# Some weight pages used unsplit in a four-phase transformer kernel: one expert page in eight, every second page of the u table

## The chip, the cores and the metric

The kernel runs on one core of a Trainium2 chip. The metric is the device time of one execution in microseconds (us). Before the change it is 3914.66 us, the median of 3 runs (3913.98 to 3925.19).

Names of the profile: PE is TensorE's matmuls, PEld its weight loads, DVE is VectorE, ACT is ScalarE, POOL is GpSimd, SP is the engine that issues loads. PEclk is the clock granted to TensorE as a share of its full speed.

## The reference

512 tokens of width 1024 go through two layers: attention, a mixture of 32 experts, a state-space model beside a second attention, and a PEER feed-forward. All inputs are float32. The change touches the mixture and the PEER part:

```
def expert_block(args):            # a block of tokens of expert e
    xe, e = args
    gu = xe @ w_gate_up[e] + b_gate_up[e]
    g = jnp.minimum(gu[:, :D_FF], SWIGLU_LIMIT)
    u = jnp.clip(gu[:, D_FF:], -SWIGLU_LIMIT, SWIGLU_LIMIT)
    act = (u + 1.0) * (g * jax.nn.sigmoid(SWIGLU_ALPHA * g))
    return act @ w_down[e] + b_down[e]

# PEER: 8 heads, 16 best of 128 x 128 experts for each token
s_top, i_top = lax.top_k(scores, PEER_TOPK)
best_s, pos = lax.top_k(cand_s, PEER_TOPK)
expert_idx = jnp.take_along_axis(cand_i, pos, axis=-1)
gates = jax.nn.softmax(best_s, axis=-1)
u_sel = u_tab[i_blk]
act = jax.nn.gelu(jnp.einsum('td,thkd->thk', h_blk, u_sel))
w = g_blk * act
out = jnp.einsum('thk,thkd->td', w, v_tab[i_blk])
```

## The kernel before

The program has four phases, one after the other on the same engines: attention (to about 490 us), experts (490 to 1852), state-space model and second attention (1852 to 2464), and PEER (from 2464). Nearly all instructions are recorded through one helper, so they carry line 84 (`Timed.call`); they are told apart by their tiles' names.

**Pages.** Weights come as pages of 128 x 1024 float32 (512 KB), loaded on SP's queue (`WStream.load`, L213) into a buffer `wr`. `WStream.split1` (L217) makes two buffers of each: `wh`, its rounding to the short float32r form, copied by ScalarE, and `wl` = `wr` - `wh`, a subtraction on VectorE or, where the stream's function `eng` says so, on GpSimd. `Kern.mm3` (L167) then multiplies exactly enough with three products: high by high, high by low, low by high. `wr`, `wh` and `wl` are buffers of one pool, which come free when their last reader is done; `ahead` (L238) and `get` (L265) load and split a number of pages ahead of use.

**Experts** (`Expert`, L1216 to L1322; `expert_stream`, L1349; `phase2`, L1375). An expert has 24 pages in the stream: 8 gate/up pages of its first half of columns, the 8 down pages of the expert before it, 8 gate/up pages of its second half. A page's product goes to two PSUM banks of 128 x 512 (`gu` or `dn`), three products each, so six matmuls a page. The 128 tokens of an expert are gathered by GpSimd (`xg`), transposed by TensorE and split (`transpose_x`, L1248: `exh`, `exl`); the activations likewise (`transpose_act`, L1286: `ath`, `atl`). Expert number `HOME` has a second block of 128 tokens, multiplied with the same pages; so 33 blocks are computed from 32 experts' pages. A loop for still more blocks (`Overflow.rest`, L1515) is in the program and is run zero times with these inputs. Every sixth page's `wl` is GpSimd's (L1372). The order of everything is written out in `phase2`: page by page, with the other steps at set page numbers.

**PEER, first stage (the u stage, 2464 to 3390).** `norm_T` (L1834) transposes and splits the normed input into `HT`. A stream of 16 query pages and 128 pages of the u table follows (L2234 to L2238). A query page gives 24 products of 512 columns; a u page (`uchunk`, L2297) gives 24 products of 384 columns (three blocks of 128 tokens) into a bank `ft`, which ScalarE turns into `us` and stores to DRAM (`Sd`). Beside this run `select` (L2320), which picks the 16 best of 50 candidate pairs for each head (a one-hot `oh` of 128 x 800, made by VectorE, multiplied with the indices `ci` at L2352 and reduced), and `gates` (L2387), which builds for each token one-hots `oa` and `oB` of 128 columns and multiplies them on TensorE (`G`), in float32 without a split. Three in four `oB` are VectorE's, the fourth is ScalarE's. The fourth block of tokens takes another way: `gathered` (L2445) fetches rows of the tables with indirect DMAs from POOL's queue and adds them up on VectorE.

The order of the u stage is made by `race` (L99): it interleaves these lanes by a table of estimated durations (`Clock`, L33). The same estimates choose, through `Clock.either` (L42), VectorE or GpSimd for each `wl` of a u page and for each multiplication of `oh`. The order and the choice are fixed when the program is built.

**PEER, second stage (the v stage, 3390 to 3917).** `vphase` (L2504) goes through 128 pages of the v table, each split as above, with 18 products of 512 columns into six banks `out` that stay open to the end. Pages of this phase come from a pool of 10 buffers (`open_pages`, L2629).

Of the kernel before, what the change touches and what calls it, by code (L numbers as in the profile page):

```python
# [15 lines left out]
ALU = mybir.AluOpType  # L16
# [16 lines left out]
class Clock:  # L33
    """Estimates when each engine gets done with what has been emitted for it; race() orders the steps of several lanes by it."""
# [4 lines left out]
    def __init__(self):  # L39
        self.start()  # L40

    def either(self, n, bias=0.0):  # L42
        """the one of VectorE and GpSimdE that gets done first with so many columns"""
        cost = [max(self.free[e], self.floor) + self.FIXED[e] + n * self.ELEM[e] for e in ("vector", "gpsimd")]
        return "vector" if cost[0] + bias < cost[1] else "gpsimd"
# [17 lines left out]
class Timed:  # L63
    """An engine whose instructions are told to the clock."""
# [34 lines left out]
def race(clock, *gens):  # L99
    """Interleaves lanes, the step that comes due first first. A lane may yield the time its next step has to wait for;  # L100
    else that is the end of its last step."""
# [94 lines left out]
class WStream:  # L196
    """Weight pages: loaded ahead, split into exact float32r halves ahead of their use."""

    def __init__(self, K, srcs, load_ahead, split_ahead, queue=None, shape=None, eng=None, late=False):
        self.eng = eng or (lambda i: None)  # L200
        self.K, self.srcs = K, list(srcs)
# [15 lines left out]
    def split1(self):  # L217
        if self.isp < len(self.srcs):
# [3 lines left out]
            self.raw[self.isp] = None  # L222
            hi = self.K.page(F32R, shape=self.shape, name="wh")
# [8 lines left out]
    def low(self):  # L232
        """the low halves of what has been split."""
# [12 lines left out]
    def lane(self, ahead, n=None):  # L246
        """splits as a lane of its own, so many pages ahead of the use."""
# [11 lines left out]
    def next(self):  # L259
        """get(), when it has been split."""  # L260
# [15 lines left out]
def weave(*gens):  # L276
    """gens: (generator, steps per unit of time, start); interleaves their steps."""
# [28 lines left out]
def phase1(K):  # L306
# [36 lines left out]
    # first modulation by blocks of columns, so that the first products start early  # L343
# [24 lines left out]
    # row norms of x, the scaled rows' transpose  # L368
# [14 lines left out]
    def mod_block(k):  # L383
        """sum over the rows of w_ada of one block of columns, shift and scale."""
# [54 lines left out]
    def product(bs, k, w):  # L439
        """one row block's part of a half chunk: two blocks of tokens to a bank."""  # L440
# [8 lines left out]
    def normed(c, half):  # L449
        """queries and keys with their heads' norms."""  # L450
# [19 lines left out]
    def drain(c, half, bs):  # L470
        """bs: the blocks of tokens in PSUM, pairs of them or one with all columns."""
# [22 lines left out]
    def take(**n):  # L494
        """waits until so much of the space is free, in the order of the program."""
# [23 lines left out]
    # the first chunk, as the blocks of the modulation come in  # L519
# [37 lines left out]
    def prep(c0, p, out):  # L557
        """q^T and k^T of a pair of heads of 64, split; the gains go with q."""
# [20 lines left out]
    def scores(qk, biases, den, es):  # L579
        """exponentials of the scores of two heads, less each row's maximum, and their sums."""  # L580
# [29 lines left out]
    def weigh(todo, new):  # L610
        """todo: per head its exponentials, the split values' columns, and PSUM [query, block, columns] or the output's place."""
# [50 lines left out]
    def out_pair(b, k, r=slice(0, P)):  # L662
        """a pair's output, transposed in PSUM, split for the output projection."""
# [9 lines left out]
    def pair_a(p):  # L673
# [25 lines left out]
        # each head with the values of both; its own half of the rows is kept  # L699
# [78 lines left out]
    def mods2():  # L778
        """gate and second modulation as rows, broadcast over the partitions."""
# [50 lines left out]
    # output projection: first with the differential heads, then with the others  # L830
# [30 lines left out]
    def projects():  # L861
        """output projection: the differential heads' part, that of the first pairs of the others, and what is left with the second norm"""
# [25 lines left out]
    def third(tb):  # L888
        """the last part of the projection, the residual's squares"""
# [1755 lines left out]
```

## Time and profile before

| | |
|---|---|
| median of 3 runs | 3914.66 us |
| profiled execution, its span | 3917.8 us |
| PE busy | 3450.1 us, 88% |
| DVE busy | 3368.7 us, 86% |
| ACT busy | 1848.5 us, 47% |
| POOL busy | 1761.6 us, 45% |
| DMA, mean | 231 GB/s |

The profile gives one execution, on the hardware profiler's clock; its own time is its span, 3917.8 us, 3.1 us above the median of the runs. A busy time is a sum over instructions. Where an instruction stands still inside itself, waiting for a port or for data, that is in its busy time too. Matmuls are pipelined: a matmul's own duration is longer than the spacing to the next, so the cost of one is read from the time that many take. A float32 product that is not of the rounded halves is recorded as two matmuls.

### The profile page before, as it was taken

To read this page: it belongs to the slowest core of one execution; us is meant where nothing else is said; L and a number is where in the kernel's file an instruction comes from. 1 tells how busy PE (TensorE), PEld (TensorE's weight loads), DVE (VectorE), ACT (ScalarE), POOL (GpSimd) and SP (SyncE) were. 2 spreads that over 40 slices of the span, in tenths; PEclk is the share of its full clock that TensorE was granted. 3 is DMA by queue.
4 is the path that set the end of the run, shared out by engine and by line. 5 is a ranking of instruction groups with operands and counts; after the bars stand their busy time and mean duration, and the time that the engine had idled before them with its cause. 6 is when DMAs were issued, how large, how long until landed. Compare 5 with 4: busy or idle time off the path is not lost. (4 is left out here: it accounts for less than half of the span.)

```text
span 3917.8 us, 52046 instructions
## 1 busy us (share of the span) xinstructions
PE 3450.1 (88%) x17053; PEld 2921.3 (75%) x17053; DVE 3368.7 (86%) x5450; ACT 1848.5 (47%) x2684; POOL 1761.6 (45%) x1021
## 2 busy tenths in 40 slices
PE   6887689888989999998489899899688889999999
PEld 6776577666778777776377777788678789988887
DVE  7887799999997999997688774589999996598888
ACT  3334266665765767675234343433334445333333
POOL 6554434323332333332344340266666564555554
PEclk8878799999999999999699999899888999999999
DMA  6224379888987999997511122366568686999997
GB/s 213 85 83 146 127 263 316 299 301 282 321 293 245 320 338 328 338 330 254 175 49 49 49 61 89 124 220 214 187 209 262 210 298 211 328 343 340 344 342 264
DMA packets 453989, 906.04 MB, mean 231 GB/s; under 512 B 37810, under 2 KB 188978, under 8 KB 453586
## 3 DMA queue, kind: packets, MB, share of 16 engines
q1 hardware_dynamic: 333488, 692.66, 52.1%
q0 software_dynamic: 46368, 151.03, 11.0%
q10 hardware_dynamic: 73858, 59.00, 4.5%
q8 instruction: 135, 2.21, 0.2%
q14 instruction: 140, 1.15, 0.1%
HBM read 845.42 MB, written 74.96 MB: 235 GB/s over the span
## 5 line engine op out<-in xcount | busy, mean ns | idle before, releaser
L84 DVE TENSOR_TENSOR wl<-wr,wh 128x1024 fp32r<-128x1024 f32 x855 | 1210.4, 1445 | 113.9 <-ACT wh L84 106.5
L84 ACT CAST wh<-wr 128x1024 fp32r<-128x1024 f32 x1133 | 1133.3, 1049 | 206.1 <-POOL wl L84 53.4
L84 POOL TENSOR_TENSOR wl<-wr,wh 128x1024 fp32r<-128x1024 f32 x278 | 714.3, 2570 | 809.8 <-ACT wh L84 695.1
L84 PE MATMUL ft<-HT,wh 128*128 128x384 f32 (+1 forms) x2304 | 637.6, 359 | 2.4 <-ACT wh L84 2.0
L84 PE MATMUL gu<-wl,exh 128*128 128x512 f32 x1056 | 426.9, 404 | 88.1 <-DVE wl L84 81.6
L84 PE MATMUL out<-wh,HT 128*128 128x512 f32 x1536 | 473.2, 389 | 1.8 <-ACT HT L84 1.5
L84 PEld LDWEIGHTS ft<-HT,wh 128*128 128x128 f32 x2304 | 438.8, 200 | 12.5 <-ACT wh L84 2.4
L84 PE MATMUL ft<-HT,wl 128*128 128x384 f32 (+1 forms) x1152 | 409.6, 356 | 34.6 <-POOL wl L84 24.0
L84 PE MATMUL gu<-wh,exh 128*128 128x512 f32 x1056 | 423.6, 401 | 0.0
L84 PE MATMUL gu<-wh,exl 128*128 128x512 f32 x1056 | 417.4, 395 | 0.0
L84 PEld LDWEIGHTS out<-wh,HT 128*128 128x128 f32 x1536 | 288.2, 188 | 62.3 <-ACT HT L84 1.8
L84 PEld LDWEIGHTS gu<-wl,exh 128*128 128x128 f32 x1056 | 201.3, 191 | 162.8 <-DVE wl L84 116.0
L84 PE MATMUL out<-wl,HT 128*128 128x512 f32 x768 | 298.8, 389 | 0.0
L84 PEld LDWEIGHTS ft<-HT,wl 128*128 128x128 f32 x1152 | 228.6, 198 | 46.9 <-POOL wl L84 28.6
L84 DVE TENSOR_SCALAR oa<-iota,rt 128x128 f32<-128x128 f32 x384 | 227.1, 595 | 19.8 <-PE G L84 19.6
L84 PE MATMUL qkv<-wl,hTh 128*128 128x256 f32 (+1 forms) x736 | 227.1, 308 | 14.5 <-DVE wl L84 11.9
L84 PE MATMUL qkv<-wh,hTh 128*128 128x256 f32 (+1 forms) x736 | 234.7, 319 | 2.0 <-ACT wh L84 2.0
L84 PEld LDWEIGHTS gu<-wh,exh 128*128 128x128 f32 x1056 | 201.6, 191 | 44.5 <-issue 1.5
L84 PEld LDWEIGHTS gu<-wh,exl 128*128 128x128 f32 x1056 | 201.3, 191 | 39.9
L84 PE MATMUL qkv<-wh,hTl 128*128 128x256 f32 (+1 forms) x736 | 226.2, 307 | 2.5 <-DVE hTl L84 2.5
L84 PE MATMUL dn<-wl,ath 128*128 128x512 f32 x528 | 210.2, 398 | 11.0 <-DVE wl L84 9.6
L2454 POOL DMA_INDIRECT ug<-in_peer_v,et x128 | 153.9, 1202 | 139.5 <-DVE x L84 74.0
(482 smaller groups left out, 7054.1 us busy)
## 6 DMA issues: line engine op xcount, KB each, us to landing
wr<-in_w_gate_up SPq DMA_DIRECT2D x512, 512.0 KB
wr<-in_w_down SPq DMA_DIRECT2D x256, 512.0 KB
wr<-in_u_t SPq DMA_DIRECT2D x128, 512.0 KB
wr<-in_peer_v SPq DMA_DIRECT2D x128, 512.0 KB
wr<-in_w_in SPq DMA_DIRECT2D x68, 512.0 KB
wada<-in_w_ada SPq DMA_DIRECT2D x48, 512.0 KB
Sd<-us ACTq DMA_DIRECT2D x128, 192.0 KB
Gd<-gst ACTq DMA_DIRECT2D x12, 2048.0 KB
```

What stands on the lines that cost most here:

```text
L84: return f(*a, **kw)
L2454: nc.gpsimd.indirect_dma_start(out=r, out_offset=None, in_=tab, in_offset=bass.IndirectOffsetOnAxis(ap=et[:, m:m + 1], axis=0), bounds_che ...
```

## The change

- `WStream` gets a function `whole`: for a page that it names, nothing is split and the raw page is handed to the user.
- Experts: pages with number 5 of each eight are used unsplit (`WHOLE`), 3 of 24 in each expert. `gu_page` and `down_page` then do one plain float32 product for each bank instead of three. The input's slice for it is kept unsplit (`Expert.keep`, an extra ScalarE copy `un` of 128 x 128). The function `eng` is gone, so all low halves of the experts are VectorE's. The loop in `Overflow.rest` likewise.
- u table: odd pages, 64 of 128, are used unsplit, with one float32 product of 384 columns for each of the eight parts instead of three. The unsplit input stands in `HW`, which `norm_T` fills with eight more ScalarE activations. The other u pages' low halves are all VectorE's.
- The multiplication of `oh` is always VectorE's.
- `us` has three buffers instead of four; the pool of the last phase has 8 page buffers instead of 10.
- Comments and docstrings are dropped (left out below).

```diff
 class WStream:
-    def __init__(self, K, srcs, load_ahead, split_ahead, queue=None, shape=None, eng=None, late=False):
+    def __init__(self, K, srcs, load_ahead, split_ahead, queue=None, shape=None, eng=None, late=False, whole=None):
         self.eng = eng or (lambda i: None)
+        self.whole = whole or (lambda i: False)
...
             self.raw[self.isp] = None
+            if self.whole(self.isp):
+                self.done.append((r,))
+                self.isp += 1
+                return
             hi = self.K.page(F32R, shape=self.shape, name="wh")
...
+WHOLE = (5,)
...
             K.split(b, self.xT[0][:, s], self.xT[1][:, s])
+            self.keep(self.xw, b, half)
+
+    def keep(self, out, b, half):
+        for k in WHOLE:
+            if k // 4 == half:
+                out[k] = self.K.small([P, P], tag=f"un{k}", bufs=6)
+                self.K.nc.scalar.copy(out[k], b[:, k % 4 * P:(k % 4 + 1) * P])
...
     def gu_page(self, k, w):
         s = slice(k * P, (k + 1) * P)
         for i in range(2):
+            if len(w) == 1:
+                self.K.nc.tensor.matmul(self.gu[i], self.xw[k], w[0][:, i, :], start=False, stop=k == KC - 1)
+                continue
...
     def down_page(self, k, w):
...
+            if len(w) == 1:
+                self.K.nc.tensor.matmul(self.dn[i], self.aw[k], w[0][:, hs], start=k == 0, stop=k == KC - 1)
+                continue
...
-    K.ws = WStream(K, srcs, MLA[0], 3, eng=lambda i: K.nc.gpsimd if i % 6 == 5 else None)
+    K.ws = WStream(K, srcs, MLA[0], 3, whole=lambda i: i % KC in WHOLE)
...
-def norm_T(K, x, gcol, outs, scratch_gain=True):
+def norm_T(K, x, gcol, outs, whole=None):
...
+        if whole is not None:
+            n = whole.shape[2]
+            nc.scalar.activation(whole[:, k, :], b[:, 0:n], AF.Copy, scale=gcol[:, k:k + 1])
...
-    ws = WStream(K, [(flat if c else feat)(n) for c, n in order], 3, 2, eng=lambda i: getattr(nc, K.clock.either(D, VB)) if order[i][0] else None)
+    ws = WStream(K, [(flat if c else feat)(n) for c, n in order], 3, 2, whole=lambda i: order[i][0] and order[i][1] % 2)
...
+    HW = K.const([P, KC, TD], name="HW")
+    xn = norm_T(K, K.x3, gcol, hTk, HW)
...
         for k in range(KC):
+            if len(w) == 1:
+                nc.tensor.matmul(b[:, 0:n], w[0][:, k, :], HW[:, k, 0:n], start=k == 0, stop=k == KC - 1)
+                continue
...
-        s = K.small([P, TD], tag="us", bufs=4)
+        s = K.small([P, TD], tag="us", bufs=3)
...
-                getattr(nc, K.clock.either(TK * NCAND, VB2)).tensor_tensor(out=oh, in0=oh, in1=ci[:, h, None, :].to_broadcast(sh), op=ALU.mult)
+                v.tensor_tensor(out=oh, in0=oh, in1=ci[:, h, None, :].to_broadcast(sh), op=ALU.mult)
...
-            K.open_pages(K.ctx4, 10)
+            K.open_pages(K.ctx4, 8)
```

What the change does to the order of instructions, at three places. TensorE, page 5 of the first expert's down product. `dn` are the two banks, `wh` and `wl` the halves of the page, `ath` and `atl` those of the activations, `wr` the raw page, `un` the slice kept unsplit. Before, page 5 and the first product of page 6:

```order
L84 MATMUL dn_4652<-wh_4672,ath_4217 128x512
L84 MATMUL dn_4652<-wl_4673,ath_4217 128x512
L84 MATMUL dn_4652<-wh_4672,atl_4218 128x512
L84 MATMUL dn_4653<-wh_4672,ath_4217 128x512
L84 MATMUL dn_4653<-wl_4673,ath_4217 128x512
L84 MATMUL dn_4653<-wh_4672,atl_4218 128x512
L84 MATMUL dn_4652<-wh_4692,ath_4217 128x512
```

and now, from the last product of page 4 on:

```order
L84 MATMUL dn_4635<-wh_4642,atl_4220 128x512
L84 MATMUL dn_4634<-wr_4556,un_4596 128x512
L84 MATMUL dn_4635<-wr_4556,un_4596 128x512
L84 MATMUL dn_4634<-wh_4670,ath_4219 128x512
L84 MATMUL dn_4634<-wl_4671,ath_4219 128x512
```

Six products became two, which need the raw page and no low half.

POOL in the u stage, late, where the gathers (`ug`, indirect DMAs) run. Before, they stand between low halves and multiplications:

```order
L2454 DMA ug_24511<-in_peer_v,et_22053 128x1024
L84 TENSOR_TENSOR wl_24537<-wr_24364,wh_24536 128x1024
L2454 DMA ug_24570<-in_peer_v,et_22053 128x1024
L2454 DMA ug_24600<-in_peer_v,et_22053 128x1024
L84 TENSOR_TENSOR wl_24606<-wr_24431,wh_24605 128x1024
L2454 DMA ug_24659<-in_peer_v,et_22053 128x1024
L84 TENSOR_TENSOR wl_24665<-wr_24472,wh_24664 128x1024
L84 TENSOR_TENSOR oh_24699<-oh_24699,ci_24519 128x800
```

and now the gathers are alone:

```order
L2483 DMA ug_23613<-in_peer_v,et_21394 128x1024
L2483 DMA ug_23657<-in_peer_v,et_21394 128x1024
L2483 DMA ug_23716<-in_peer_v,et_21394 128x1024
L2483 DMA ug_23739<-in_peer_v,et_21394 128x1024
L2483 DMA ug_23781<-in_peer_v,et_21394 128x1024
```

In the whole program POOL's subtractions `wl` went from 278 to 27 (all 27 in the first phase) and its multiplications `oh` from 28 to 0.

VectorE at the same place, in a selection: `bpf` are the positions found, `x` is the sum of gathered rows, `ex` the reduced indices. Before:

```order
L84 CAST bpf_24579<-bp_24578 128x128
L84 TENSOR_TENSOR oh_24699<-bpf_24579,iotac_21953 128x800
L84 SCALAR_TENSOR_TENSOR x_21923<-ug_24350,sv_22824,x_21923 128x1024
L84 TENSOR_TENSOR oh_24741<-bpf_24579,iotac_21953 128x800
L84 TENSOR_TENSOR oh_24741<-oh_24741,ci_24519 128x800
L84 SCALAR_TENSOR_TENSOR x_21923<-ug_24511,sv_22824,x_21923 128x1024
L84 TENSOR_REDUCE ex_24520<-oh_24699 128x16
```

and now:

```order
L84 CAST bpf_23636<-bp_23635 128x128
L84 TENSOR_TENSOR oh_23736<-bpf_23636,iotac_21285 128x800
L84 TENSOR_TENSOR oh_23736<-oh_23736,ci_23596 128x800
L84 SCALAR_TENSOR_TENSOR x_21255<-ug_23452,sv_22081,x_21255 128x1024
L84 TENSOR_TENSOR oh_23744<-bpf_23636,iotac_21285 128x800
L84 TENSOR_TENSOR oh_23744<-oh_23744,ci_23596 128x800
L84 TENSOR_TENSOR wl_23748<-wr_23620,wh_23747 128x1024
```

Every multiplication stands right behind its one-hot now, and a low half `wl` of a u page stands in VectorE's order too.

## Rows read from the trace of the kernel before

**Rows 1.** Windows view: stretch, length, busy us of each engine, PEclk, DMA share, GB/s.

```profile
490.00:1852.00 1362.00, 1248.90 (x5562) 991.85 (x5560) 1292.10 (x1599) 897.75 (x1036) 460.70 (x198) 0.98 0.88 304
2464.00:3390.00 926.00, 808.10 (x4426) 766.29 (x4427) 796.45 (x1958) 364.48 (x645) 550.83 (x303) 0.93 0.68 222
3390.00:3917.00 527.00, 522.53 (x2304) 431.98 (x2303) 461.94 (x425) 189.50 (x256) 290.75 (x233) 1.00 0.93 329
1600.00:1800.00 200.00, 186.05 (x849) 149.67 (x849) 195.77 (x199) 142.47 (x166) 70.18 (x30) 1.00 0.95 330
2689.00:3214.00 525.00, 430.26 (x2307) 410.57 (x2308) 515.12 (x1078) 203.58 (x382) 342.61 (x192) 0.90 0.70 229
```

**Rows 2.** Groups by shape, 490 to 1852: count, busy us, mean ns, idle before, releasers.

```profile
L84 DVE TENSOR_TENSOR wl<-wr,wh 128x1024 fp32r<-128x1024 f32 x637 | 900.8, 1452 | 20.1 <-ACT wh L84 17.2 <-DMA ybuf<-y,dst 1.8
...
L84 PE MATMUL gu<-wl,exh 128*128 128x512 f32 x1056 | 426.9, 404 | 88.1 <-DVE wl L84 81.6 <-POOL wl L84 6.1
...
L84 POOL TENSOR_TENSOR wl<-wr,wh 128x1024 fp32r<-128x1024 f32 x128 | 344.1, 2689 | 516.6 <-ACT wh L84 473.8 <-PE dn L84 15.7 <-PE gu L84 14.2
...
L84 PE MATMUL dn<-wl,ath 128*128 128x512 f32 x528 | 210.2, 398 | 11.0 <-DVE wl L84 9.6 <-POOL wl L84 1.2
...
L84 DVE SCALAR_TENSOR_TENSOR act<-swu,swt 128x512 f32<-128x512 f32 x66 | 80.2, 1214 | 3.1
...
L84 DVE SCALAR_TENSOR_TENSOR swt<-gu,swr 128x512 f32<-128x512 f32 x66 | 45.1, 684 | 2.4 <-ACT swr L84 2.4
```

**Rows 3.** Timeline (start, duration, engine) around 2902 us, and VectorE's at 1303 us.

```profile
2901.86 0.28 DVE L84 TENSOR_SCALAR oB<-iota,rt 128x128 f32<-128x128 f32 x1
2902.06 0.34 DVE L84 TENSOR_SCALAR oa<-iota,rt 128x128 f32<-128x128 f32 x1
...
2902.16 2.53 POOL L84 TENSOR_TENSOR wl<-wr,wh 128x1024 fp32r<-128x1024 f32 x1 [6.21 <-ACT wh L84]
2902.32 2.46 DVE L84 TENSOR_SCALAR oB<-iota,rt 128x128 f32<-128x128 f32 x1
...
1303.31 2.36 DVE L84 TENSOR_TENSOR wl<-wr,wh 128x1024 fp32r<-128x1024 f32 x2
```

**Rows 4.** Groups by shape, 2464 to 3390 (columns as in rows 2).

```profile
L84 PE MATMUL ft<-HT,wl 128*128 128x384 f32 x1024 | 358.0, 350 | 24.1 <-POOL wl L84 24.0
L84 POOL TENSOR_TENSOR wl<-wr,wh 128x1024 fp32r<-128x1024 f32 x123 | 302.6, 2461 | 185.9 <-ACT wh L84 142.3 <-issue 30.2 <-PE G L84 8.3
...
L84 DVE TENSOR_SCALAR oa<-iota,rt 128x128 f32<-128x128 f32 x384 | 227.1, 595 | 19.8 <-PE G L84 19.6 <-ACT rt L84 0.2
L84 DVE TENSOR_SCALAR oB<-iota,rt 128x128 f32<-128x128 f32 x288 | 163.5, 568 | 0.0
...
L84 PE MATMUL G<-oB,oa 128*128 128x128 f32 x768 | 129.3, 304 | 67.3 <-DVE oB L84 62.4 <-ACT oB L84 3.5
...
L84 ACT ACTIVATE us<-ft 128x384 f32<-128x384 f32 x128 | 62.9, 491 | 240.5 <-PE ft L84 236.5 <-DMA wr<-in_u_t 2.1 <-issue 1.7
L84 POOL TENSOR_TENSOR oh<-oh,ci 128x800 f32<-128x800 f32 x28 | 59.4, 2126 | 89.3 <-DVE oh L84 86.3 <-DMA wr<-in_u_t 3.0
...
L84 DVE TENSOR_TENSOR oh<-oh,ci 128x800 f32<-128x800 f32 x4 | 4.0, 992 | 0.1
```

**Rows 5.** The chain of waits near the end of the u stage: start, us, what.

```profile
3256.55 0.89 PE G L84 x8
3257.44 4.16 PE ft L84 x24
```

**Rows 6.** Timeline of PE in the third phase, float32 products of 512 columns.

```profile
2203.96 1.90 PE L84 MATMUL y<-tmp,cz 128*32 128x512 f32 x4
```

**Rows 7.** Timeline of PE, the bias products that open two successive experts.

```profile
1706.03 0.63 PE L84 MATMUL gu<-bg,pls 128*128 128x512 f32 x2
...
1745.34 0.63 PE L84 MATMUL gu<-bg,pls 128*128 128x512 f32 x2
```

**Rows 8.** Waits of SP's DMA queue, 3391 to 3900: us in total, times, longest.

```profile
SPq L213 <- PE out L84: 347.0, 118, 3.2
```

More of the change, by code (lines that the diff above doesn't have):

```diff
@@ L1221, in __init__ @@
         self.sel = sel
+        self.xw, self.aw = {}, {}
     def slots(self):
@@ L1293, in transpose_act @@
         K.split(b, self.aT[0][:, s], self.aT[1][:, s])
+        self.keep(self.aw, b, c)
     def down_start(self):
@@ L1521, in rest @@
             srcs = [gu_src(self.wgu, c, k) for c in range(2) for k in range(KC)] + [self.wdn[k * P:(k + 1) * P, :] for k in range(KC)]
-            ws = WStream(K, srcs, 6, 3)
+            ws = WStream(K, srcs, 6, 3, whole=lambda i: i % KC in WHOLE)
             x.slots()
@@ L2246, in hTk @@
         return HT[0][:, k, 0:n], HT[1][:, k, 0:n]
-    xn = norm_T(K, K.x3, gcol, hTk)
+    HW = K.const([P, KC, TD], name="HW")
+    xn = norm_T(K, K.x3, gcol, hTk, HW)
     ht3 = K.hold(name="ht3")
```

## The prediction, made before the change was run

> **What bounds the kernel now.** I read three things in turn: the windows view, to see which engine is full in which stage; the groups of instructions of the two stages that the change touches, for what ended TensorE's idle time and for durations; and timelines, for what an instruction costs when nothing disturbs it.
>
> The windows [rows 1] show three different limits. In the v stage (3390 to 3917) TensorE is busy 522.5 of 527 us at granted clock 1.00: the products set the pace there. In the expert stage (490 to 1852) it is busy 1248.9 of 1362, and late in it, from 1600 to 1800, VectorE is busy 195.8 of 200 us. In the u stage (2464 to 3390) TensorE is busy 808.1 of 926, and in its main stretch, from 2689 to 3214, VectorE is busy 515.1 of 525 us while the granted clock is 0.90 in the mean. So VectorE is full where TensorE is not.
>
> What TensorE waits for confirms it. In the expert stage its idle time ends with low halves: 88.1 us ahead of `gu<-wl` and 11.0 ahead of `dn<-wl`, 98.5 of them put down to `wl` [rows 2]. In the u stage 24.1 us end with a `wl` of GpSimd and 67.3 ahead of the one-hot products `G` [rows 4].
>
> But part of VectorE's busy time is no work. In the timeline around 2902 [rows 3] an `oB` takes 0.28 us and the next instruction starts 0.20 us after it, `oa` after 0.26; then GpSimd starts a `wl` of 2.53 us, and the very next `oB` takes 2.46 us: it stands until GpSimd is done. In the group the means are 595 ns for `oa` and 568 for `oB` [rows 4]. The same shows in the experts: two lows in a row take 2.36 us together, 1.18 each [rows 3], and the mean of the stage's 637 is 1452 ns [rows 2].
>
> **Prices of the two forms of product.** A product of rounded halves over 512 columns: 522.5 us by 2304 products in the v stage, 0.2268 us [rows 1]. A plain f32 product is recorded as two matmuls. Eight records of `G`, f32 over 128 columns, take 0.89 us [rows 5], 0.111 each; in proportion 0.444 for 512 columns and 0.333 for 384. An expert page (two banks) then costs 4 x 0.444 = 1.78 us where six products of halves cost 1.36: +0.42. A u page costs 16 x 0.333 = 5.33 us where the 24 products of halves take 4.16 [rows 5]: +1.17. From the other side, four f32 records `y` over 512 columns span 1.90 us [rows 6], with their pipeline's tail in it: +0.54 and +1.54. From below: at one column a cycle of 2.4 GHz, near which the 0.2268 us lie, a record that passes 512 columns twice takes 0.427 us: +0.35 and +0.96. I take 0.42 and 1.17, because `G` is the form that runs at full clock beside the same products.
>
> The Trainium skill, "FP8 and Floating Point Precision", section "TensorE Precision Notes", says that true FP32 takes four passes through the array. By that a u page would cost 4/3 of its three-product time, 5.55 us, and an expert page 1.81, and the sum would come to some 17 us more. The `G` rows put it a little lower.
>
> **Experts.** Of 24 pages an expert, 3 are now used unsplit, and all lows are VectorE's. TensorE: 96 pages, 3 of them used by two blocks of slots, so 99 x 0.42 = +41.5 us. VectorE: without GpSimd's 128 lows, what stands still goes: 900.8 - 637 x 1.18 = 149 us on the lows, and 80.2 - 66 x 0.69 = 35 on `act` (its like `swt` takes 684 ns) [rows 2]. There are 672 lows instead of 640: +32 x 1.18 = +38. So VectorE falls from 1292 to 1292 - 149 - 35 + 38 = 1146 us, under what TensorE needs, and TensorE becomes the bound: -98.5 us of waits for lows, +41.5 of products. A mean clock of 0.98 [rows 1] stands for 27 us lost; with the waits gone I give half of that back, -13, and I leave +10 for waits that stay at the ends of experts. Together **-60 us**; by the bounds of the price and of those last two terms -20 to -90.
>
> ScalarE makes 96 fewer page copies and 66 copies of a 128-column slice `un`, each under the 0.49 us of a 384-column activation [rows 4]; it is 898 of 1362 us busy [rows 1]: nothing. A page used unsplit holds its raw buffer until TensorE is past it, but takes no two others: if anything loads start earlier. That a product now waits for the load itself, with no split between, changes nothing while loads run pages ahead.
>
> **The u stage.** TensorE's own work at full clock: 128 u pages x 4.16 = 532.5; 384 query products of 512 columns x 0.2268 = 87; 768 records of `G` [rows 4] and the queries' scores, 16 x 4 x 3 products of 128 columns taken at the same price, 960 x 0.111 = 107: 726 us. Busy is 808 because the clock is at its lower level for part of the time (0.93 in the mean). The change adds 64 x 1.17 = +75: 801. Of the 926 - 808 = 118 us idle, 24.1 + 67.3 go with GpSimd's lows and the late one-hots; 26.5 stay: 827.5. VectorE: 796 - (227.1 - 384 x 0.26 = 127) - (163.5 - 288 x 0.20 = 106), both from [rows 4] with the undisturbed spacings of [rows 3], +59 lows x 1.18 = 70, +28 multiplies x 0.99 = 28 [rows 4]: 661 us, 80% of 827.5. So it no longer ends the stage. The one-hot multiply and the lows now stand in VectorE's own order, and what is queued behind them are `oa` and `oB`; their cover is the 20% that VectorE is free. The POOL queue keeps only the row gathers: they stood behind lows and multiplies (the order of POOL shows it), so they can only be earlier. HW adds eight activations of 384 columns at the stage's head, at 0.49 us each [rows 4] = +4. Together 831.5 instead of 926, **-94.5 us**; by the bounds of the price -71 to -110.
>
> The sum needs that clock: a stage whose TensorE waits less was seen at 1.00 (the v stage, 99% busy), the present one at 0.93 (87%).
>
> **The v stage.** Ten page buffers become eight. A step takes 18 x 0.2268 = 4.08 us and uses three pages, so ten buffers let a page be held 10/3 x 4.08 = 13.6 us in the mean, eight 10.9. SP, which loads, already waits 347.0 us in 118 waits for TensorE to release a page [rows 8]; so buffers are filled as soon as they come free, and what a page needs at least is below what it now gets. I take 0. Fewer `us` buffers: 0, they are copied out by ScalarE's queue within the next chunk's time.
>
> **Sum.** -60 - 94.5 = -154.5 against the profiled execution's span of 3917.8: 3763. The median of the runs, 3914.66, is 3.1 below that span, so I forecast **3760 us**.
>
> **Rivals.**
> *VectorE is simply full, and work taken back from GpSimd lengthens it* (the other side). Then `oa` at 595 ns is its real cost, the u stage, which VectorE sets, grows by 70 + 28 = 98 us, the experts by 38, HW adds 4: 3914.7 + 140 = 4055. It decides the case if one GpSimd instruction holds VectorE up by less than (98 + 38)/(128 + 123 + 28) = 0.49 us. By the means above it is (149 + 35)/128 = 1.44 us in the experts and (127 + 106)/151 = 1.54 in the u stage, and the `oB` of 2.46 us shows one such stop. Chance 0.05. The Trainium skill, "Perfetto Trace Analysis", section "Optimizing Scalar/DVE Operations", says that offloading from a saturated VectorE, even to GpSimd, may make sense; by that alone undoing it would cost what this rival says. The same passage warns that the two share a read port, so that moving work between them might not help; with that the trace agrees (2.46 us against 0.28).
>
> *DMA becomes the experts' bound.* Bytes do not change. Late experts follow each other at 1745.34 - 1706.03 = 39.31 us [rows 7] at 330 GB/s and a share of 0.95 [rows 1], 13.0 MB each; at share 1 that is 37.3 us, and my -60 asks for 39.31 x 1302/1362 = 37.6. It fits by 1%. If half or all of the experts' gain goes, 3790 to 3820, say 3805. Against it: over the whole stage the share is 0.88. Chance 0.2.
>
> *Eight buffers stretch the v stage.* If a page needs the 13.6 us that it now gets, a step becomes 13.6 x 3/8 = 5.1 us: 128 x 1.02 = +131, 3891. Against it: the waits of SP. Chance 0.07.
>
> *The change does not do what it says*: GpSimd's lows would still be there, about 3915. The order rows show them gone. Chance 0.02.
>
> **How the numbers follow.** Forecast 0.66. Its own range, by the bounds of the price and of the experts' last terms, is 3715 to 3825; with the DMA rival the range to 3850 also takes in a u stage whose one-hots wait a little still. Outside lie the two dear rivals, the fourth, and some of each tail: 0.2. A measurement of this kernel tells about 0.3%, 12 us, from no change, so 3903 to 3926 counts as the same. Faster: the forecast, the DMA rival and most of the buffers' one, 0.92; same 0.03; slower 0.05.
>
> **What would show it.** Right: no `wl` or `oh` on POOL after 490 us; means of `oa` and `oB` near 0.34 and 0.28 us; `wl` near 1.2; TensorE busy 97% of a u stage of some 830 us at clock 1.00, f32 records of 384 columns spaced 0.33; the expert stage near 1302 us with TensorE's waits for `wl` mostly gone; the v stage still near 527. Wrong: VectorE over 95% busy with the one-hots as slow as before, a v step over 4.2 us with TensorE waiting for `wr`, expert waits that end with a load, or records of 384 columns 0.4 us apart.

## The result and the profile after

The changed kernel takes 3773.68 us (median of 4 runs, 3770.63 to 3788.37) against 3914.69 before (4 runs, 3913.98 to 3925.19): ratio 0.9638, 95% interval 0.9623 to 0.9654. The forecast was 3760 in a range of 3715 to 3850; the measured time is 13.7 us above it. The profiled execution's span is 3774.0 us.

Stages are cut at the same events in both traces: the first `gu` product, the start of the last `dn`, the last product `ft<-hTl` of the third phase, the first `ft` of the fourth, the first `out`.

| stage | before, us | after, us | change | forecast |
|---|---|---|---|---|
| attention | 490.0 | 486.1 | -3.9 | 0 |
| experts | 1361.5 | 1288.2 | -73.3 | -60 |
| third phase, to its last `ft<-hTl` | 498.6 | 499.5 | +0.9 | 0 |
| from there to the fourth phase's first `ft` | 113.9 | 122.1 | +8.2 | +4 (HW) |
| u stage | 925.7 | 846.4 | -79.3 | -98.5 |
| v stage | 528.1 | 531.7 | +3.6 | 0 |
| span | 3917.8 | 3774.0 | -143.8 | -154.5 |

The attention phase has the same code in all kernels here (one of them has a page buffer fewer in it) and lay between 477.1 and 491.3 us in fourteen profiles, so its -3.9 says nothing. The windows view of the changed kernel answers to [rows 1] (stretch, length, busy us of PE, PEld, DVE, ACT, POOL, PEclk, DMA share, GB/s):

```profile
486.10:1774.30 1288.20, 1256.60 (x5363) 952.24 (x5362) 1127.81 (x1630) 821.37 (x1006) 105.28 (x70) 0.99 0.91 321
2395.90:3242.30 846.40, 816.16 (x3914) 651.19 (x3914) 651.51 (x2045) 301.37 (x580) 199.51 (x152) 0.99 0.71 244
3242.30:3774.00 531.70, 524.68 (x2304) 431.75 (x2304) 469.70 (x425) 189.63 (x256) 287.69 (x232) 1.00 0.91 325
1600.00:1750.00 150.00, 150.00 (x652) 116.01 (x651) 132.60 (x153) 103.94 (x127) 9.46 (x6) 1.00 0.98 353
```

TensorE has taken VectorE's place as the full engine: 1256.6 of 1288.2 us in the experts, 816.2 of 846.4 in the u stage, with the granted clock at 0.99 in both. VectorE is busy 88% and 77%. The groups of the experts (486 to 1775) answer to [rows 2]:

```profile
L84 DVE TENSOR_TENSOR wl<-wr,wh 128x1024 fp32r<-128x1024 f32 x669 | 784.7, 1218 | 89.3 <-ACT wh L84 88.3 <-DMA wr<-in_w_gate_up 0.5 <-issue 0.3
...
L84 PE MATMUL gu<-wl,exh 128*128 128x512 f32 x924 | 363.9, 394 | 5.1 <-DVE wl L84 4.8
...
L84 PE MATMUL dn<-wl,ath 128*128 128x512 f32 x462 | 185.1, 401 | 12.4 <-DVE wl L84 12.2
...
L84 DVE SCALAR_TENSOR_TENSOR act<-swu,swt 128x512 f32<-128x512 f32 x66 | 45.7, 692 | 2.4
```

A low half takes 1218 ns in the mean instead of 1452, `act` 692 instead of 1214, and TensorE's waits for low halves fell from 98.5 us to 17.0. No `wl` of POOL is left. The u stage (2395 to 3243) answers to [rows 4]:

```profile
L84 DVE TENSOR_SCALAR oa<-iota,rt 128x128 f32<-128x128 f32 x384 | 134.5, 356 | 4.4 <-PE G L84 4.4
...
L84 PE MATMUL G<-oB,oa 128*128 128x128 f32 x768 | 109.9, 283 | 7.8 <-ACT oB L84 7.7
...
L84 DVE TENSOR_SCALAR oB<-iota,rt 128x128 f32<-128x128 f32 x288 | 82.7, 287 | 0.0
...
L84 DVE TENSOR_TENSOR oh<-oh,ci 128x800 f32<-128x800 f32 x32 | 31.7, 992 | 1.1
```

`oa` and `oB` are at 356 and 287 ns, from 595 and 568; the 67.3 us of waits ahead of `G` are 7.8.

The two prices can now be read. In the chain of waits a u page of halves takes 4.16 us as before and an unsplit one 5.16, +1.00 (start, us, what):

```profile
3146.14 0.89 PE G L84 x8
3147.03 4.16 PE ft L84 x24
3151.19 0.89 PE G L84 x8
3152.08 5.16 PE ft L84 x16
3157.25 27.45 PE G L84 x152
```

and TensorE's timeline of an expert (start, duration) shows an unsplit page and the products around it:

```profile
1606.52 0.39 PE L84 MATMUL gu<-wh,exl 128*128 128x512 f32 x1
1606.75 1.88 PE L84 MATMUL gu<-wr,un 128*128 128x512 f32 x4
1608.07 0.80 PE L84 MATMUL gu<-wh,exh 128*128 128x512 f32 x1
1608.70 0.40 PE L84 MATMUL gu<-wl,exh 128*128 128x512 f32 x1
```

From 1606.75 to 1608.70 lie the page and one product of halves: 1.95 - 0.23 = 1.72 us, +0.36 against 1.36. Both prices lie near the forecast's lower bound, +0.35 and +0.96, which it had worked out for 512 columns passed twice in a record at 2.4 GHz.

### The profile page after: what moved, and what is told of

Same layout as the page of the kernel before. It is cut to its first block, busy times and chain, and to the rows that moved or that the text cites. A ratio compares the mean times of both kernels' runs of the same rounds, so it can differ in the third digit from the quotient of the medians.

```text
span 3774.0 us, 49950 instructions
## 1 busy us (share of the span) xinstructions
PE 3461.4 (92%) x16343; PEld 2760.9 (73%) x16343; DVE 3064.1 (81%) x5569; ACT 1713.0 (45%) x2598; POOL 1054.4 (28%) x742
## 5 line engine op out<-in xcount | busy, mean ns | idle before, releaser
L84 DVE TENSOR_TENSOR wl<-wr,wh 128x1024 fp32r<-128x1024 f32 x946 | 1161.0, 1260 | 286.2 <-ACT wh L84 265.1
L84 ACT CAST wh<-wr 128x1024 fp32r<-128x1024 f32 x973 | 972.0, 1048 | 123.2 <-DVE wl L84 51.5
L84 PE MATMUL gu<-wl,exh 128*128 128x512 f32 x924 | 363.9, 394 | 5.1 <-DVE wl L84 4.8
L84 PE MATMUL ft<-HT,wh 128*128 128x384 f32 (+1 forms) x1280 | 353.2, 357 | 11.7 <-ACT wh L84 11.7
L84 PE MATMUL gu<-wh,exl 128*128 128x512 f32 x924 | 362.5, 392 | 0.0
L84 PE MATMUL ft<-HW,wr 128*128 128x384 f32 x1024 | 345.2, 491 | 0.0
L84 PEld LDWEIGHTS ft<-HW,wr 128*128 128x128 f32 x1024 | 192.6, 192 | 120.9 <-issue 3.7
L2483 POOL DMA_INDIRECT ug<-in_peer_u,et x128 | 161.8, 1264 | 420.3 <-DVE sv L84 194.5
L84 PEld LDWEIGHTS ft<-HT,wh 128*128 128x128 f32 x1280 | 232.8, 190 | 28.1 <-ACT wh L84 11.9
L84 PE MATMUL ft<-HT,wl 128*128 128x384 f32 (+1 forms) x640 | 223.6, 349 | 14.0 <-DVE wl L84 14.0
L84 ACT ACTIVATE us<-ft 128x384 f32<-128x384 f32 x128 | 62.9, 492 | 333.5 <-PE ft L84 331.9
```

The lines of the kernel that those rows point to most:

```text
L84: return f(*a, **kw)
L2483: nc.gpsimd.indirect_dma_start(out=r, out_offset=None, in_=tab, in_offset=bass.IndirectOffsetOnAxis(ap=et[:, m:m + 1], axis=0), bounds_che ...
```

## The experiments

Diffs are against the changed kernel. "Theory A" is the forecast's mechanism: a GpSimd instruction stops VectorE, and taking GpSimd's work back is what pays. Stage times are of one profile each.

### Only the moves: every page split, all lows and multiplications on VectorE

```diff
-WHOLE = (5,)
+WHOLE = ()
...
-    ws = WStream(K, [...], 3, 2, whole=lambda i: order[i][0] and order[i][1] % 2)
+    ws = WStream(K, [...], 3, 2)
...
-    HW = K.const([P, KC, TD], name="HW")
-    xn = norm_T(K, K.x3, gcol, hTk, HW)
+    HW = None
+    xn = norm_T(K, K.x3, gcol, hTk)
...
-        s = K.small([P, TD], tag="us", bufs=3)
+        s = K.small([P, TD], tag="us", bufs=4)
...
-            K.open_pages(K.ctx4, 8)
+            K.open_pages(K.ctx4, 10)
```

> Every page split again (no unsplit page, no HW, 10 page buffers, 4 us buffers), but all low halves of the experts and of the u table and all oh multiplications on VectorE. Theory A (what pays is that GpSimd no longer stops VectorE; an unsplit page costs TensorE 0.36 us in the experts and 1.00 us in the u stage, as the changed kernel's trace shows, and gives VectorE 1.18 us it does not need): u stage 846 - 64 + some waits = 780 to 800 us with VectorE at 727 us, experts 1288 - 36 to + 10 = 1255 to 1300 with VectorE at 1241, the whole 3690 to 3720, so faster than the changed kernel. Theory B (VectorE was truly full and the unsplit pages are what pays): 279 GpSimd instructions' work added to a full VectorE at 1.0 to 1.2 us each, 4100 to 4230 us.

3757.38 us (3752.13 to 3772.42), 0.9601 of before (0.9566 to 0.9636). Theory B is out by 340 us: VectorE took the work of 279 GpSimd instructions and the kernel became 157 us faster, by the medians 16 us more than with the unsplit pages (the two intervals overlap a little). In numbers theory A missed too, by 37 us: the experts came at 1291.8, as expected, the u stage at 840.5 instead of 780 to 800.

```profile
481.10:1772.90 1291.80, 1230.75 (x5562) 989.18 (x5560) 1227.86 (x1726) 897.08 (x1036) 136.50 (x70) 0.99 0.90 320
2385.20:3225.70 840.50, 766.07 (x4426) 734.20 (x4426) 723.62 (x2109) 361.82 (x644) 209.87 (x152) 0.96 0.74 245
```

VectorE's 1227.9 and 723.6 us are what A had worked out (1241, 727), and TensorE is busy 50 us less in the u stage without f32 products, but it idles 74 us there, 24.6 of them ahead of `G` for ScalarE's `oB`. That wait is taken up below.

```profile
L84 PE MATMUL G<-oB,oa 128*128 128x128 f32 x768 | 107.0, 284 | 25.7 <-ACT oB L84 24.6 <-DVE oB L84 1.1
```

### The same with the change's buffers

```diff
-            K.open_pages(K.ctx4, 10)
+            K.open_pages(K.ctx4, 8)
```

(against the kernel just shown; `us` at 3 buffers too)

> As all_split_vector, with the last phase's 8 page buffers and 3 us buffers of the change. If the buffers make the 3.6 us by which the v stage grew and the 8 us by which the stretch between the last ft of the third phase and the first ft of the fourth grew (114 to 122 us), this kernel shows both (v stage 531 to 532, stretch 122) and all_split_vector shows neither. If HW's eight activations make the 8 us, both kernels show 114. Whole time 0 to 12 us over all_split_vector.

3789.49 us (3787.86 to 3800.51). It missed: the whole is 32 us over the other, not 0 to 12. The stretch ahead of the fourth phase is 114.0 in both, so HW makes the +8.2, not the buffers. The v stage is 531.0, as in the changed kernel. The 32 us lie where neither expectation nor forecast had looked, in the u stage: 872.3 against 840.5.

### GpSimd's work put back beside unsplit pages

```diff
-    K.ws = WStream(K, srcs, MLA[0], 3, whole=lambda i: i % KC in WHOLE)
+    K.ws = WStream(K, srcs, MLA[0], 3, eng=lambda i: K.nc.gpsimd if i % 6 == 5 else None, whole=lambda i: i % KC in WHOLE)
...
-    ws = WStream(K, [...], 3, 2, whole=...)
+    ws = WStream(K, [...], 3, 2, eng=lambda i: getattr(nc, K.clock.either(D, VB)) if order[i][0] else None, whole=...)
...
-                v.tensor_tensor(out=oh, in0=oh, ...)
+                getattr(nc, K.clock.either(TK * NCAND, VB2)).tensor_tensor(out=oh, in0=oh, ...)
```

> The changed kernel with GpSimd's work put back where pages are still split: every sixth expert page's low, and lows of the u table and oh multiplications by the planner's choice. Theory A: each GpSimd instruction stops VectorE for 1.4 to 1.5 us where it saves 1.0 to 1.2, so VectorE's busy time rises although it has less to do (means of oa and oB back over 0.45 us), TensorE's waits for low halves return in part: experts 1300 to 1340, u stage 860 to 900, the whole 3800 to 3860. Theory B: VectorE is relieved of 96 + some 60 lows, so the same or less than the changed kernel, 3700 to 3775.

3879.52 us (3874.19 to 3881.07), 0.9904 of before (0.9877 to 0.9931): theory A's direction, 20 us beyond its range. With GpSimd's share left as it was, the unsplit pages, with HW and the change's buffers, bring 1%. Windows and groups of its two stages:

```profile
485.20:1821.70 1336.50, 1275.20 (x5363) 951.00 (x5362) 1170.31 (x1534) 821.25 (x1006) 363.46 (x166) 0.99 0.88 309
2443.70:3344.10 900.40, 831.20 (x3914) 663.75 (x3914) 652.13 (x1956) 301.50 (x580) 414.66 (x241) 0.96 0.68 229
```

```profile
L84 DVE TENSOR_TENSOR wl<-wr,wh 128x1024 fp32r<-128x1024 f32 x573 | 796.7, 1423 | 114.3 <-ACT wh L84 105.1 <-issue 5.6 <-POOL wl L84 2.3
...
L84 PE MATMUL gu<-wl,exh 128*128 128x512 f32 x924 | 369.7, 400 | 37.6 <-DVE wl L84 34.9 <-POOL wl L84 2.0
...
L84 DVE SCALAR_TENSOR_TENSOR act<-swu,swt 128x512 f32<-128x512 f32 x66 | 76.0, 1152 | 2.3
```

VectorE makes 96 lows fewer in the experts than in the changed kernel, 96 x 1.218 = 117 us of work, and is busy 1170.3 us instead of 1127.8: each of GpSimd's 96 cost it (117 + 42.5)/96 = 1.66 us. In the u stage it makes 62 lows and 27 multiplications fewer, 102 us, and is as busy as in the changed kernel, 652.1 us against 651.5: 1.15 us for each. Moving an instruction to GpSimd cost VectorE as much as keeping it, or more. TensorE's longer waits are for VectorE's own lows (34.9 us), not for GpSimd's (2.0).

### More unsplit pages in the experts, fewer of the u table

```diff
-WHOLE = (5,)
+WHOLE = (2, 5)
...
-... whole=lambda i: order[i][0] and order[i][1] % 2)
+... whole=lambda i: order[i][0] and order[i][1] % 4 == 1)
...
-            K.open_pages(pages, 30)
+            K.open_pages(pages, 29)
```

> Two expert pages in eight unsplit (one page buffer fewer in the first three phases, 29, to make room for the slices), one u page in four unsplit instead of two. Theory A: in both stages TensorE sets the pace, so experts 1288 + 99 x 0.36 = 1318 to 1326, u stage 846 - 32 = 810 to 820, the whole 3765 to 3785. Theory B: VectorE sets the pace, so experts fall by up to 96 x 1.18 = 113 us and the u stage grows by up to 38. If the experts are bound by the loads, they stay at 1285 to 1292.

3795.14 us (3793.91 to 3803.46), 10 us beyond theory A's range. The experts are 1312.2 us with TensorE busy 1290.8: it sets the pace, not VectorE (1030.5) and not the loads. A second unsplit page costs 24 us; the first one cost nothing (1288.2 against 1291.8 with none). The u stage missed: 852.1 instead of 810 to 820, again with only eight buffers.

### What held the u stage: an issue on ScalarE's queue

The traces of these kernels show ScalarE standing before `oB` with nothing that it waits for. The worst case in the changed kernel and in the one with all pages split and eight buffers (ScalarE's timeline; ACTq lines are DMA issues):

```profile
2883.82 0.55 ACTq L2442 DMA_DIRECT2D Gd<-gst  x1
2888.36 0.49 ACT L84 ACTIVATE us<-ft 128x384 f32<-128x384 f32 x1 [4.58 <-PE ft L84]
2888.89 9.65 ACTq L2330 DMA_DIRECT2D Sd<-us  x1
2898.59 0.40 ACT L84 ACTIVATE oB<-iota,rt 128x128 f32<-128x128 f32 x1 [9.73 <-issue]
```

```profile
2847.99 0.55 ACTq L2442 DMA_DIRECT2D Gd<-gst  x1
...
2851.42 12.95 ACTq L2330 DMA_DIRECT2D Sd<-us  x1
2864.42 0.40 ACT L84 ACTIVATE oB<-iota,rt 128x128 f32<-128x128 f32 x1 [13.03 <-issue]
```

A store of `us` (Sd, 192 KB), usually 0.33 us to issue, takes 9.65 and 12.95 us when it is the first behind a store of one-hot products (Gd, 2 MB) on the same queue, and ScalarE's next `oB`, the `G` that needs it and TensorE stand behind it. It is not so each time: before the change four of the twelve first stores took under 1 us. Issues of Sd over 1 us sum to 32.8 us before, 42.0 after, 66.8 with all pages split, 86.2 with eight buffers besides. Eight more runs bear on it.

Moving those stores, one line:

```diff
-        nc.scalar.dma_start(out=Sd[j], in_=s)
+        nc.gpsimd.dma_start(out=Sd[j], in_=s)
```

> The changed kernel with one queue changed: the stores of us (Sd) go to GpSimd's queue instead of ScalarE's. In the changed kernel's u stage ten of the 128 Sd issues take over 1 us (42.0 us together, up to 9.65), each the first behind a 2 MB store of one-hot products (Gd) on the same queue, and ScalarE's next oB stands behind it. Theory Q (this queue stop is part of what the u stage took beyond the forecast): no stop on ScalarE is left, TensorE's waits for ScalarE's oB (7.7 us) go and the gates' tail shrinks, u stage 8 to 25 us shorter than 846, the whole 3750 to 3768. Rival N (TensorE and VectorE catch up whatever ScalarE does, or the stores only move their stop to GpSimd, where the gathers stand behind it): u stage within 5 us of 846 or longer, the whole 3770 or more.

3768.04 us (3764.12 to 3774.69), 0.9609 of before (0.9595 to 0.9622): as theory Q expected, at its edge. The u stage is 837.4 us, and TensorE no longer waits ahead of `G`:

```profile
L84 PE MATMUL G<-oB,oa 128*128 128x128 f32 x768 | 109.2, 282 | 0.0
```

The whole gained less than the 9 us of the u stage, and the intervals of 0.9638 and 0.9609 lie end to end (from 0.9623, to 0.9622); the stage shows it, the whole only just.

The same with all u pages split, ten page buffers and four `us` buffers (the experts as changed):

> Experts of the change (one page in eight unsplit), every u page split with its low on VectorE, 10 page buffers, 4 us buffers, and the Sd stores on GpSimd's queue. The same u stage with these stores on ScalarE's queue took 840.5 us with 66.8 us of long issues and 24.6 us of TensorE's waits for ScalarE's oB. Theory Q: u stage 805 to 830, the whole 3715 to 3745, the best so far. Rival N: u stage 836 or more, the whole 3747 or more.

3731.61 us (3729.9 to 3737.39), 0.9523 of before (0.951 to 0.9536), the best of all kernels and 1.1% under the changed one. The u stage is 811.3 us instead of 840.5:

```profile
2386.20:3197.50 811.30, 759.72 (x4425) 728.70 (x4425) 721.40 (x2109) 350.74 (x643) 298.26 (x277) 0.97 0.74 254
```

```profile
L84 PE MATMUL ft<-HT,wl 128*128 128x384 f32 x1024 | 349.1, 341 | 19.8 <-DVE wl L84 19.7
...
L84 PE MATMUL G<-oB,oa 128*128 128x128 f32 x768 | 102.9, 279 | 1.1 <-DVE oB L84 1.1
```

And with eight page buffers (`open_pages(K.ctx4, 8)`), nothing else changed:

> usplit_10_sd_pool with 8 page buffers instead of 10 in the last phase, nothing else. With the Sd stores on ScalarE's queue, eight buffers had a split u stage of 872 us and 86 us of long Sd issues, ten 840 and 67. If the buffers acted only through these issues on ScalarE's queue, the u stage stays within 5 us of 811 and the whole within 8 of 3732. If three buffers for each split page are themselves too few in eight, the u stage is 825 to 845 and the whole 3745 to 3770, with ScalarE's copies waiting for buffers (wh behind wl or ft).

3741.98 us (3736.71 to 3744.35); u stage 820.1. Both expectations missed, by a little, since both hold in part: eight buffers cost 32 us with the stores on ScalarE's queue and 9 without. Most of their price was paid through the queue. The rest, which the intervals of the two wholes do not tell apart (0.951 to 0.9536, 0.9527 to 0.957), goes with ScalarE's page copies: with eight buffers they wait 113.0 us behind TensorE's `ft` and 97.6 behind VectorE's `wl`, with ten hardly.

Are the `us` buffers part of it?

```diff
-        s = K.small([P, TD], tag="us", bufs=4)
+        s = K.small([P, TD], tag="us", bufs=3)
```

(against the kernel with only the moves)

> all_split_vector with 3 us buffers instead of 4, nothing else (10 page buffers). The kernels with 4 us buffers had a split u stage of 840.5 us (10 pages), those with 3 had 872 (8 pages) and 862 (11 pages). If the us buffers matter (a us has to be stored before its buffer is free, and an Sd store behind a Gd store lands late), this kernel shows 855 to 870 us and the whole 3772 to 3795. If the page buffers matter, 838 to 844 and 3750 to 3765.

3760.84 us (3751.89 to 3772.06), u stage 841.3 against 840.5: no.

### The rest of the u stage: buffers, the fourth one-hot, the planner's pace

Experts as changed, all u pages split (no HW, as shown above), 11 page buffers:

```diff
-    ws = WStream(K, [...], 3, 2, whole=lambda i: order[i][0] and order[i][1] % 2)
+    ws = WStream(K, [...], 3, 2)
...
-            K.open_pages(K.ctx4, 8)
+            K.open_pages(K.ctx4, 11)
```

> The changed kernel's experts (one page in eight unsplit), but every u page split with its low on VectorE, no HW, and 11 page buffers in the last phase (3 us buffers). Theory P (split pages take three buffers each, and too few of them hold up the split, and behind it on ScalarE the fourth oB): eight buffers gave a u stage of 872 us and ten 840, so eleven give 825 to 836 with TensorE's waits ahead of G under 20 us; the whole 3735 to 3752. Theory V (with all lows VectorE is the bound of this u stage, and buffers no longer matter beyond ten): u stage 838 to 843, the whole 3747 to 3760.

3798.02 us (3781.85 to 3801.46): both theories missed. Eleven buffers are worse than ten, with a u stage of 862.3 us, long issues of 80.1 us and a v stage of 544.2. The queue's stops, 13 us more than with ten, may be part of the 22 us more in the u stage; why they grow with one buffer more, and what lengthens the v stage, is open.

The same with the fourth `oB` on VectorE (`UPACE, BV = 5.1, 4`):

> As usplit_11, with the fourth oB of each four made by VectorE too instead of ScalarE (96 pairs of ScalarE activations less, 96 one-hots of 0.20 us more on VectorE: +19). Theory P: TensorE's waits for ScalarE's oB (24.6 us with ten buffers, 43.8 with eight) vanish and ScalarE's queue no longer holds one-hots behind copies that wait for a page: u stage 5 to 25 us shorter than usplit_11. Theory V: VectorE is full from the selections on, so 5 to 19 us longer.

3776.49 us (3766.14 to 3779.62), u stage 847.3 against 862.3: theory P. VectorE has 17 us more to do and the stage is 15 shorter, since TensorE no longer depends on the engine whose queue stops.

The changed kernel with that edit alone:

> The changed kernel with the fourth oB on VectorE. There TensorE waits only 7.7 us for ScalarE's oB and VectorE has 195 us free in the u stage: u stage 2 to 10 us shorter if those waits go, 3 to 6 us longer if the pace of the gates' tail (152 records of G in 27.5 us after the last paced u page, 10.6 us over their price, made at VectorE's pace) decides.

3767.7 us (3762.81 to 3771.6), u stage 838.2 against 846.4: 8 us shorter, as when the stores are moved, though the long issues are still there (49.5 us). Here too the stage shows it and the whole does not: 0.9617 (0.9604 to 0.963) overlaps with the changed kernel's interval.

The changed kernel with `UPACE, BV = 5.6, 3`:

> The changed kernel with the planner's spacing of u pages at 5.6 us instead of 5.1, so that one-hots and G products come earlier relative to u pages in the fixed order. If the gates' tail (152 records of G with no u page between them) costs the 10.6 us over its price because the planner paces u pages faster than the gates, the tail shrinks to under 40 records and the u stage falls by 5 to 12 us, to 834 to 841. If the tail is only where waits happen to show, no change within 4 us, or longer because VectorE becomes the bound earlier.

3790.93 us (3788.8 to 3793.09), u stage 861.7. The tail, the last 152 records of `G` in the changed kernel, is gone: no more than 16 stand together near the end. But the stage is 15 us longer. With the gates earlier, TensorE waits 24.0 us ahead of `G` for ScalarE's `oB` instead of 7.7, long issues sum to 62.7 us, and the granted clock is 0.97 in the mean instead of 0.99. So nothing is won by this way of removing the tail; what the tail costs by itself, the run does not show.

## Why the prediction was right, and which of its steps were off

**The mechanism.** Right, and the other side's rival is refuted twice: by the kernel with only the moves (faster, where it asked for slower) and by the one that undoes only them (3879.5). The point from which it would have decided was 0.49 us of VectorE's time for each GpSimd instruction; the runs show 1.15 to 1.66. The Trainium skill, "SBUF — State Buffer", section "SBUF: two separate sides", says that VectorE and GpSimd share one port pair as an exclusive lock, taken by VectorE instructions that use both port pairs or have two inputs in SBUF, and that whichever starts second stands still for the other's whole instruction. With that the trace agrees: the `oB` of 2.46 us starts 0.16 us after GpSimd's `wl` of 2.53 [rows 3]. Which ports an `oB` uses, no run here shows.

**Experts, forecast -60, measured -73.3.** VectorE was to fall to 1146 us and fell to 1127.8. TensorE's busy time was to grow by 28.5 us (products +41.5, clock -13) and grew by 8.1, 20 less; its idle time was to fall by 88.5 and fell by 81.4, 7 less, since waits for low halves were to fall to some 10 and fell to 17.0. The term that was mis-sized is thus TensorE's busy time. Of the 20 us the price of the unsplit page, +0.42 taken and +0.36 measured, makes 99 x 0.06 = 6. A record lasts 0.39 us where the spacing is 0.23, so a wait fewer also takes a tail of 0.16 us out of busy time; TensorE's waits fell from 85 to 32, so that is some 8 us, by an estimate that was not tried. The rest is not placed.

**u stage, forecast -98.5, measured -79.3.** VectorE was to be at 661 us and is at 651.5; idle time of TensorE was to be 26.5 and is 30.2. The price was again off in its favour, +1.00 for +1.17: 64 x 0.17 = 11 us. So at the measured price TensorE's own work is 790 us and its busy time 816: 26 us are missing, and they lie in busy time. Two steps failed. One is "their cover is the 20% that VectorE is free", a mean over the stage. The last 152 records of `G` stand together and take 27.45 us where 152 x 0.111 is 16.9, so TensorE counts as busy 10.6 us longer than its records' price; VectorE, which makes most of their one-hots, is busy 25.9 of these 27.45 us. The other is the full clock: in three stretches of 40 us the granted clock was 0.90, 0.91 and 0.87 in the mean (of its two levels, 1.2 and 2.4 GHz), and TensorE was busy 102.8 us in them for records that cost 93.1 at full clock. In the second of them VectorE is busy 39.1 of 40 us. These two make 20 of the 26 us; the rest is not placed. The windows, columns as in [rows 1]:

```profile
3157.25:3184.70 27.45, 27.45 (x153) 21.33 (x153) 25.91 (x112) 20.71 (x53) 0.00 (x0) 1.00 0.53 161
2396.00:2436.00 40.00, 36.71 (x166) 29.96 (x167) 16.69 (x51) 12.36 (x18) 0.00 (x0) 0.90 0.35 116
2676.00:2716.00 40.00, 32.37 (x135) 25.07 (x135) 39.14 (x92) 13.11 (x24) 10.99 (x8) 0.91 0.65 216
2876.00:2916.00 40.00, 33.77 (x155) 26.59 (x154) 26.35 (x124) 11.73 (x24) 9.02 (x8) 0.87 0.80 283
```

The step on cover also looked at VectorE only, and took no note that the fourth one-hot is made by ScalarE, whose queue can stand. The row was there, `G` waiting 3.5 us for ScalarE's `oB` before. This part lies in TensorE's idle time: taking away that dependence, in two ways, brought it from 30.2 us to 21.1 and 21.5 and gave back 9.0 and 8.2, while busy time stayed at 816. The forecast's best bound for the stage, -110, is also a little off: -94.5 - 64 x 0.21 is -108.

**HW, forecast +4, measured +8.2.** The step counted eight activations by their duration. In the timeline each `HW` waits 0.82 us for VectorE's `HT` of the same bank and then takes 0.58, and ScalarE's next `HT` follows only then:

```profile
2380.94 0.68 ACT L84 ACTIVATE HT<-xnT,ffng 128x512 fp32r<-128x512 f32 x1
2382.44 0.58 ACT L84 ACTIVATE HW<-xnT,ffng 128x384 f32<-128x384 f32 x1 [0.82 <-DVE HT L84]
2382.92 0.68 ACT L84 ACTIVATE HT<-xnT,ffng 128x512 fp32r<-128x512 f32 x1
```

A round is 1.98 us; in the kernel without HW it is 0.85 (`HT` at 2378.06, 2378.91, 2379.77), and 8 x 1.13 = 9.

**v stage, forecast 0, measured +3.6.** With eight buffers it was 528.3 to 534.5 us in eight kernels, with ten 527.6 to 530.6 in four: 0 to 4 us. The rival of 5.1 us a step is out. But the argument on buffers was made for one stage of a pool that serves two: in the u stage eight buffers cost 32 us when every page is split. The unsplit pages, which take one buffer and not three, may have hidden that; the changed kernel with ten buffers was not run.

**DMA rival.** From 1600 to 1750 loads run at 353 GB/s and a share of 0.98, with TensorE busy 150.0 of 150 us: the 1% of room that the forecast counted held.

**What the sum did not say.** It came within 0.4%, and that is in part luck: the experts gained 13 us more than forecast, the u stage 19 less, HW cost 4 more, and 3.9 lie in the attention phase. Nor does it say that the unsplit pages were not needed. The moves alone give -157 us; unsplit pages, HW and eight buffers together give 16 of them back by the medians, with intervals that overlap a little. For the u table it is clear of the noise: with the stores on GpSimd's queue in both, the u stage as changed gives 0.9609 (0.9595 to 0.9622), all its pages split, without HW and with the buffers of before, 0.9523 (0.951 to 0.9536). The forecast's own numbers could have shown it for the experts: without unsplit pages TensorE is spared 41.5 us and VectorE has 1146 + 96 x 1.18 = 1259, so both fit in about 1260 us, no more than the 1302 forecast. It was measured at 1291.8, level with the 1288.2 of the changed kernel. No such variant was costed.

## What to carry to other kernels

Before work is shared between VectorE and GpSimd, compare the mean of VectorE's instructions with the shortest of the same kind beside idle GpSimd: where it is double, as for `oa` and `oB` here, GpSimd's help may cost VectorE more than it takes off. A form of product that needs fewer operand buffers can look good because it makes room elsewhere; run the variant without it. And when an engine both computes on the critical path and issues DMAs, look at the durations of its issues, not only at its waits.

## What the runs showed of the hardware that was not expected

A DMA issue on ScalarE's queue that follows a 2 MB store on that queue held the engine up to 13.83 us, in a kernel where the issue usually takes 0.33; on GpSimd's queue the same stores took at most 0.74 us to issue. Nothing in the waits view names it, the time appears as "issue". A float32 product ran at 0.32 us for 384 columns and record, 5.16 us for a page where three products of halves take 4.16, 1.24 times. The Trainium skill, "FP8 and Floating Point Precision", section "TensorE Precision Notes", gives four passes for it, by which the weight page would take 4/3 of its three products, an estimate of 5.55 us; the trace shows less, and decides. And eleven page buffers were slower than ten, which stays unexplained.
